# An encoder layer on one core: the parts of the first value column, gate2's way through DRAM, the last columns and the first loads are laid out anew

## The chip, the cores and the metric

The kernel runs on one core of a Trainium2 chip. The metric is the device time of one execution in microseconds (us). The core has TensorE (PE, with its weight loads as PEld), VectorE (DVE), ScalarE (ACT), GpSimd (POOL, hardly used here) and SyncE (SP). All DMAs of this kernel are issued by SP, in one order; an issue that has to wait holds all issues behind it.

## The reference

One layer of a bidirectional encoder, 256 tokens of width 2048, all in float32:

```
mod = SiLU(c) @ W_ada + b_ada -> shift1, scale1, gate1, shift2, scale2, gate2   (each 1 x 2048)
h = x * (1 + scale1) + shift1
x = LayerNorm(alpha * x + gate1 * Mixer(h))
h = x * (1 + scale2) + shift2
x = LayerNorm(alpha * x + gate2 * PEER(h))
```

The Mixer is an input projection, a bidirectional state-space scan beside a short gated convolution, and an output projection. PEER chooses 16 of 128 x 128 single-neuron experts per head by product keys; the kernel turns that into dense work: for each of 128 columns of 128 experts, u = h @ expert_u, a gate matrix G times gelu(u), and the sum over all columns of that product times expert_v.

## The kernel before

Float32 products are made of three matmuls on parts: a weight half (128x1024, 512 KB, "a raw half" in the text) is loaded into `raw`, ACT rounds it to `hi` (L78), and DVE takes the difference `lo` (L81). Each of raw, hi and lo has three buffers in the pool `stream`. A scheduler places each instruction by its priority, and weights are brought forward by a priority offset, so that loads run some halves ahead of their matmuls.

The stages in order of time, from the trace: adaLN's first two parts and the first quarter of the input projection (loads of w_ada and w_inA by turns), the rest of the Mixer, output projection and first LayerNorm, queries and the choice of experts, **expert_u** (128 columns, to 1815.6), **expert_v** (128 columns, 1817 to 2537), and the second LayerNorm (`finish`, to the end).

In expert_u the gates lie in GA, 128 columns as two tiles: columns below FIRST in one and the rest in the other. Each column's gelu is multiplied into its column of GA (L845). For expert_v a pair of columns is split into the parts ah and al (`a_pair`, L119 on ACT and L120 on DVE). These tiles are in a pool that takes over the memory of h2h and h2l, the parts of h that all matmuls of expert_u read. Each column is then 24 matmuls of 128x512 (L878 hi with ah, L879 hi with al, L881 lo with ah) over two halves, all into eight PSUM banks (two blocks of tokens by four blocks of 512 outputs) that are summed over all columns.

Beside expert_v run:

- sixteen steps of gate2 (`ada_step`): two loads of w_ada (512 KB each, tile `big`), a multiplication with row sum on DVE for each (L152), and at the end `ada_sum` (L158, L159) that makes a column of `mod` out of each step's sums. gate2 then stands with 128 values in each of 16 columns, across partitions, and is wanted as a row, the same on all partitions (`g2b`). It is stored to DRAM (`g_d`, L914) and loaded back as a broadcast (L915).
- the last LAST columns of expert_v, loaded into `big` and split into `old`, which takes over the memory of the first tile of GA. They are kept so that, at the end, the banks can be finished one after another, and a bank's `finish` (times g2b at L939, plus residual `ax` with row sum at L940, squares) can run beside the next bank's matmuls. The statistics of a block of 128 tokens, two more operations for each 512 outputs (L959, L960) and the store (L961) follow.

At the start, step d of the loop over 16 blocks of the width first loads adaLN's weights of step d + 1 (four loads, `ada_load`, L281), then splits two halves of w_inA and multiplies.

Of the kernel before, what the change touches and what calls it, by code (L numbers as in the profile page):

```python
# [34 lines left out]
LAG = 3  # L35
FIRST = 66
LAST = 4


@with_exitstack  # L40
def layer_kernel(ctx, tc, I, out, dbg=None):
# [27 lines left out]


    def wsplit(src, pool=stream, width=1024, ahead=600, after=None):

        with tc.high_priority(offset=ahead):
            raw = pool.tile([P, 1024], F32, name="raw", tag="raw", bufs=3)[:, :width]
            nc.sync.dma_start(raw, src)
            hi = pool.tile([P, 1024], F32R, name="hi", tag="hi")[:, :width]
            with tc.issue_after(after[0]) if after else nullcontext():
                A.activation(hi, raw, AF.Copy)  # L78
            lo = pool.tile([P, 1024], F32R, name="lo", tag="lo")[:, :width]
            with tc.issue_after(after[1]) if after else nullcontext():  # L80
                V.tensor_tensor(lo, raw, hi.bitcast(F32), op=ALU.subtract)  # L81
        c = lambda t: t.rearrange("p (k c) -> p k c", c=P)
        return c(hi), c(lo)
# [256 lines left out]
    V.memset(bones[:64, :64], 1.0)  # L340
    V.memset(bones[64:, 64:], 1.0)
    for d in range(ND):
        if d + 1 < ND:
# [6 lines left out]
        for half in range(2):  # L350
            wh, wl = wsplit(I["w_inA"][d, half], width=NA * 64, ahead=0)
            for i in range(NA // 2):
                k = half * NA // 2 + i
                mm3(first[k // 2][:, k % 2], wh[:, i], wl[:, i], h2h[:, d], h2l[:, d], False,
                    d == ND - 1 and k % 2 == 1)
            for _ in range(n // 2 if half == 0 else n - n // 2):
                unit_b(*units.pop(0))
# [437 lines left out]
    with ExitStack() as p4:  # L795
# [32 lines left out]
        with ExitStack() as p4a:  # L828
# [11 lines left out]
            for e2 in range(STAGE):  # L840
                nc.sync.dma_start(gel_d[e2], act_chunk(e2, wk, 1, step))
        wk = pool(p4, "wk4b")
        for e2 in range(STAGE, NE):
            ge = act_chunk(e2, wk, 2)
            behind = V.tensor_tensor(GA(e2)[:, 0], GA(e2)[:, 0], ge, op=ALU.mult).ins  # L845
            if e2 - STAGE < STAGE:
# [3 lines left out]
                with tc.issue_after(behind):  # L850
                    V.tensor_tensor(GA(k)[:, 0], GA(k)[:, 0], gb, op=ALU.mult)

    stR.close()


    with ExitStack() as p5:
# [41 lines left out]
        for e2 in range(NE - LAST):  # L898
            if e2 % 2 == 0:
                ah, al = a_pair(e2)  # L900
            if e2 == FIRST:
                old = gp.tile([P, FIRST, S], F32R, name="old", tag="GA0")
            for half in range(2):
                wh, wl = (w.rearrange("p k c -> p (k c)") for w in wsplit(I["expert_v"][e2, half]))
                for lo in range(2):
                    for j in range(2):
                        js = slice(j * 512, (j + 1) * 512)
                        for tb in range(2):
                            mm_v(tb, 2 * half + j, ah[:, e2 % 2], al[:, e2 % 2], wh[:, js], wl[:, js], lo, e2 == 0, False)
            if e2 % 6 == 5 and e2 < 96:  # L910
                ada_step(scb5, raw5[:2], 5, e2 // 6)
            if e2 == 100:
                ada_sum(5, slice(0, ND))
                nc.sync.dma_start(g2_d.rearrange("d p -> p d"), mod[:, 5])  # L914
                nc.sync.dma_start(g2b, bass.AP(tensor=g2_d.tensor, offset=g2_d.offset, ap=[[0, P], [1, D]]))  # L915
            if e2 >= 112:
                next(last, None)
# [5 lines left out]
        for rows, n, tag in ((lng, 0, "hi"), (lnb, 1, "lo")):  # L923
            for half in range(2):
                row = stream.tile([P, 1024], F32, name="lnrow", tag=tag)
                nc.sync.dma_start(row, bass.AP(tensor=I["ln2"].tensor, offset=I["ln2"].offset + n * D + half * 1024,
                                               ap=[[0, P], [1, 1024]]))
                rows += [row[:, :512], row[:, 512:]]

        def finish(tb):  # L930
# [3 lines left out]
            for c in range(4):  # L934
                r = rows5[tb][c]
                yield
                ax = stream.tile([P, 1024], F32, name="ax", tag="raw", bufs=3)[:, :512]
                nc.sync.dma_start(ax, ax_d[tb, :, c * 512:(c + 1) * 512])
                V.tensor_tensor(r, banks[tb][c], g2b[:, c * 512:(c + 1) * 512], op=ALU.mult)  # L939
# [95 lines left out]
```

## Time and profile before

| | before |
|---|---|
| median of three runs | 2547.92 us (2544.36 to 2559.14) |
| profiled execution | 2552.61 us |
| its span in the trace | 2550.7 us |
| mean clock granted to PE | 0.984 of full speed |
| PE busy | 2424.6 us, 95% of the span |
| DVE, ACT busy | 1862.2 us (73%), 1381.3 us (54%) |
| DMA queue with all loads and stores | 67.3% of 16 engines' time |

The span is the time from the first to the last instruction of the profiled execution; the profiled execution's own time has some 1.9 us around it. Times in views are in us from the start of the span. A row's "idle before" is what its engine waited just ahead of it, with the instruction that released it. The engine is busy when an instruction runs; matmuls overlap their successors, so the distance from one start to the next counts, which is 0.2285 us in the undisturbed value stage.

### The profile page before, as it was taken

How to read it: one execution, taken by the hardware profiler on the slowest of the kernel's cores; microseconds unless marked ns; L12 is line 12 of the kernel's file. 1: busy time of each engine (PE TensorE's matmuls, PEld its weight loads, DVE VectorE, ACT ScalarE, POOL GpSimd, SP SyncE). 2: the span in 40 equal slices, each digit the busy share in tenths (PEclk: the TensorE clock that was granted, in tenths of full speed). 3: DMA queues.
4: the chain of work that ended last, by engine and by line, in shares of the span. 5: the costliest groups of instructions: out<-in, count | busy, mean ns of one | idle time of the engine just before them, and what ended most of it. 6: DMA issues, size and time to landing. Idle time of an engine off the chain costs nothing.

```text
span 2550.7 us, 44290 instructions
## 1 busy us (share of the span) xinstructions
PE 2424.6 (95%) x17122; PEld 2248.3 (88%) x17122; DVE 1862.2 (73%) x3255; ACT 1381.3 (54%) x2506; POOL 0.9 (0%) x7
## 2 busy tenths in 40 slices
PE   5889999999999899999999999999998999999997
PEld 5889888888899799999999999999886888888886
DVE  8788888989887799898888855555675555645545
ACT  3435476656444554499999944444443444544442
POOL 0000000000000000000000000000000000000000
PEclk9999999999999899999999999999999999999999
DMA  9886766778887565355666666666788655655554
GB/s 356 313 297 236 260 217 224 235 260 280 267 291 259 196 206 181 116 181 193 199 195 200 198 218 219 218 217 219 257 307 274 217 194 190 223 192 193 193 190 149
DMA packets 183252, 575.67 MB, mean 226 GB/s; under 512 B 22209, under 2 KB 44929, under 8 KB 182657
## 3 DMA queue, kind: packets, MB, share of 16 engines
q1 hardware_dynamic: 183042, 572.85, 67.3%
q8 instruction: 134, 2.20, 0.3%
q14 instruction: 76, 0.62, 0.1%
HBM read 560.10 MB, written 12.66 MB: 225 GB/s over the span
## 4 chain that ended last, share of the span: by engine, by line
PE 67%; DMA 15%; DVE 12%; ACT 3%; issue 2%; SPq 1%; DVEq 0%; ACTq 0%
PE ps_u L91 9%; PE ps_u L92 9%; PE ps_u L93 9%; PE ps_v L879 8%; PE ps_v L881 8%; PE ps_v L878 8%; DVE lo L81 5%; DMA adaw<-in_w_ada_dram 4%; DMA raw<-in_w_in_dram 3%; DMA big<-in_w_ada_dram 2%; ACT hi L78 2%; DVE adaw L152 2%; DMA raw<-in_w_inA_dram 2%; PE ps_q L93 2%; PE ps_q L92 2%
## 5 line engine op out<-in xcount | busy, mean ns | idle before, releaser
L81 DVE TENSOR_TENSOR lo<-raw,hi 128x1024 fp32r<-128x1024 f32 (+1 forms) x804 | 972.1, 1212 | 506.8 <-ACT hi L78 504.7
L78 ACT ACTIVATE hi<-raw 128x1024 fp32r<-128x1024 f32 (+1 forms) x804 | 843.6, 1051 | 884.6 <-PE ps_v L879 302.1
L91 PE MATMUL ps_u<-h2h,hi 128*128 128x256 f32 x2048 | 568.7, 278 | 0.0
L92 PE MATMUL ps_u<-h2l,hi 128*128 128x256 f32 x2048 | 568.1, 277 | 0.0
L93 PE MATMUL ps_u<-h2h,lo 128*128 128x256 f32 x2048 | 568.1, 277 | 0.0
L878 PE MATMUL ps_v<-hi,ah 128*128 128x512 f32 x992 | 390.1, 393 | 9.9 <-ACT hi L78 8.1
L879 PE MATMUL ps_v<-hi,al 128*128 128x512 f32 x992 | 390.7, 394 | 1.2 <-DVE al L120 1.2
L91 PEld LDWEIGHTS ps_u<-h2h,hi 128*128 128x128 f32 x2048 | 386.2, 189 | 0.0
L92 PEld LDWEIGHTS ps_u<-h2l,hi 128*128 128x128 f32 x2048 | 384.6, 188 | 0.0
L93 PEld LDWEIGHTS ps_u<-h2h,lo 128*128 128x128 f32 x2048 | 384.5, 188 | 0.0
L881 PE MATMUL ps_v<-lo,ah 128*128 128x512 f32 x992 | 268.9, 393 | 0.8 <-DVE lo L81 0.8
L878 PEld LDWEIGHTS ps_v<-hi,ah 128*128 128x128 f32 x992 | 187.5, 189 | 52.3 <-ACT hi L78 8.9
L879 PEld LDWEIGHTS ps_v<-hi,al 128*128 128x128 f32 x992 | 187.7, 189 | 43.0 <-DVE al L120 1.6
L91 PE MATMUL ps_in<-h2h,hi 128*128 128x256 f32 x768 | 222.3, 289 | 3.0 <-DVE mod L159 2.2
L881 PEld LDWEIGHTS ps_v<-lo,ah 128*128 128x128 f32 x992 | 186.8, 189 | 42.0 <-DVE lo L81 2.0
L93 PE MATMUL ps_in<-h2h,lo 128*128 128x256 f32 x768 | 217.6, 283 | 2.3 <-DVE lo L81 2.3
L152 DVE SCALAR_TENSOR_TENSOR adaw<-adaw,scb 128x1024 f32<-128x1024 f32 x160 | 193.1, 1219 | 35.3 <-DMA adaw<-in_w_ada_dram 35.0
L92 PE MATMUL ps_in<-h2l,hi 128*128 128x256 f32 x768 | 217.6, 283 | 0.0
L809 ACT ACTIVATE o<-eq,gT 128x128 fp32r<-128x128 f32 x512 | 161.4, 388 | 0.0
L91 PEld LDWEIGHTS ps_in<-h2h,hi 128*128 128x128 f32 x768 | 146.6, 191 | 9.0 <-issue 4.2
L93 PEld LDWEIGHTS ps_in<-h2h,lo 128*128 128x128 f32 x768 | 147.1, 191 | 4.6 <-DVE lo L81 2.9
L93 PE MATMUL ps_o<-y,lo 128*128 128x256 f32 x512 | 145.6, 284 | 5.0 <-DVE lo L81 4.9
(285 smaller groups left out, 3975.0 us busy)
## 6 DMA issues: line engine op xcount, KB each, us to landing
raw<-in_expert_u_dram SPq DMA_DIRECT2D x256, 512.0 KB, 4.5
raw<-in_expert_v_dram SPq DMA_DIRECT2D x248, 512.0 KB, 3.9
adaw<-in_w_ada_dram SPq DMA_DIRECT2D x160, 512.0 KB, 6.0
raw<-in_w_in_dram SPq DMA_DIRECT2D x110, 512.0 KB, 5.0
raw<-in_w_out_dram SPq DMA_DIRECT2D x64, 512.0 KB, 4.3
raw<-in_w_query_dram SPq DMA_DIRECT2D x64, 512.0 KB, 3.9
raw<-in_w_inB_dram SPq DMA_DIRECT2D x44, 512.0 KB, 4.4
big<-in_w_ada_dram SPq DMA_DIRECT2D x32, 512.0 KB, 5.6
```

Of the source, the lines that this page charges most:

```text
L78: A.activation(hi, raw, AF.Copy)
L81: V.tensor_tensor(lo, raw, hi.bitcast(F32), op=ALU.subtract)
L91: T.matmul(ps, wh, mh, start=start, stop=False)
L92: T.matmul(ps, wh, ml, start=False, stop=False)
L93: T.matmul(ps, wl, mh, start=False, stop=stop)
L152: V.scalar_tensor_tensor(w, w, 0.5, scb[:, cs], op0=ALU.mult, op1=ALU.mult, accum_out=macc[:, half, part % 2, d:d + 1])
L809: A.activation(o2[:, k], eq[:, i, 1].bitcast(F32), AF.Copy, scale=gT[:, k, t0 + i:t0 + i + 1])
L878: T.matmul(banks[tb][c], ah[:, ts], vh, start=start, stop=False)
L879: T.matmul(banks[tb][c], al[:, ts], vh, start=False, stop=False)
L881: T.matmul(banks[tb][c], ah[:, ts], vl, start=False, stop=stop)
```

## The change

Five places are edited.

1. The first tile of GA holds 98 columns instead of 66 (FIRST), and 6 columns instead of 4 (LAST) are kept for the end; their loads begin at column 110 instead of 112.
2. Column 0 of GA is split into tiles of its own, a0h and a0l, at column 72 of expert_u (STAGE is 64), in a pool of their own. Column 0 of expert_v uses these.
3. gate2 is summed step by step and stored in sixteen stores of 128 elements, each written one step behind its sum; the broadcast load comes at column 104.
4. The residual `ax` is loaded in four loads of 128x1024 ahead of `finish`, in place of eight of 128x512 within it.
5. The first two halves of w_inA are loaded ahead of the loop, and so ahead of adaLN's weights of step 1.

```diff
@@ -33,8 +33,8 @@
 TURNS = (0, 1, 7, 2, 8), (3, 9, 4, 10, 5, 11, 6), (12, 13, 14, 15)
 WHOLE = range(3, 43, 3)
 LAG = 3
-FIRST = 66
-LAST = 4
+FIRST = 98
+LAST = 6
 
 
 @with_exitstack
@@ -68,11 +68,16 @@
     lnp = const.tile([P, 2, ND], F32, name="lnp")
 
 
+    def wload(src, pool=stream, width=1024):
+        raw = pool.tile([P, 1024], F32, name="raw", tag="raw", bufs=3)[:, :width]
+        nc.sync.dma_start(raw, src)
+        return raw
+
     def wsplit(src, pool=stream, width=1024, ahead=600, after=None):
 
         with tc.high_priority(offset=ahead):
-            raw = pool.tile([P, 1024], F32, name="raw", tag="raw", bufs=3)[:, :width]
-            nc.sync.dma_start(raw, src)
+            raw = src if pool is None else wload(src, pool, width)
+            pool = pool or stream
             hi = pool.tile([P, 1024], F32R, name="hi", tag="hi")[:, :width]
             with tc.issue_after(after[0]) if after else nullcontext():
                 A.activation(hi, raw, AF.Copy)
@@ -339,6 +344,7 @@
     V.memset(bones, 0.0)
     V.memset(bones[:64, :64], 1.0)
     V.memset(bones[64:, 64:], 1.0)
+    raws = [wload(I["w_inA"][0, half], width=NA * 64) for half in range(2)]
     for d in range(ND):
         if d + 1 < ND:
             ada_load(d + 1)
@@ -348,7 +354,8 @@
             units += [(d // 4 - 1, u) for u in range(NB // 2)]
         n = -(-len(units) // (4 - d % 4))
         for half in range(2):
-            wh, wl = wsplit(I["w_inA"][d, half], width=NA * 64, ahead=0)
+            wh, wl = (wsplit(raws[half], None, NA * 64, 0) if d == 0 else
+                      wsplit(I["w_inA"][d, half], width=NA * 64, ahead=0))
             for i in range(NA // 2):
                 k = half * NA // 2 + i
                 mm3(first[k // 2][:, k % 2], wh[:, i], wl[:, i], h2h[:, d], h2l[:, d], False,
@@ -839,6 +846,7 @@
 
             for e2 in range(STAGE):
                 nc.sync.dma_start(gel_d[e2], act_chunk(e2, wk, 1, step))
+        a0 = pool(ctx, "a0")
         wk = pool(p4, "wk4b")
         for e2 in range(STAGE, NE):
             ge = act_chunk(e2, wk, 2)
@@ -849,6 +857,10 @@
                 nc.sync.dma_start(gb, gel_d[k])
                 with tc.issue_after(behind):
                     V.tensor_tensor(GA(k)[:, 0], GA(k)[:, 0], gb, op=ALU.mult)
+            if e2 == STAGE + 8:
+
+                a0h, a0l = (a0.tile([P, S], F32R, name=n) for n in ("a0h", "a0l"))
+                split(a0h, a0l, GA(0)[:, 0])
 
     stR.close()
 
@@ -898,6 +910,7 @@
         for e2 in range(NE - LAST):
             if e2 % 2 == 0:
                 ah, al = a_pair(e2)
+            ahs, als = (a0h, a0l) if e2 == 0 else (ah[:, e2 % 2], al[:, e2 % 2])
             if e2 == FIRST:
                 old = gp.tile([P, FIRST, S], F32R, name="old", tag="GA0")
             for half in range(2):
@@ -906,14 +919,17 @@
                     for j in range(2):
                         js = slice(j * 512, (j + 1) * 512)
                         for tb in range(2):
-                            mm_v(tb, 2 * half + j, ah[:, e2 % 2], al[:, e2 % 2], wh[:, js], wl[:, js], lo, e2 == 0, False)
-            if e2 % 6 == 5 and e2 < 96:
-                ada_step(scb5, raw5[:2], 5, e2 // 6)
-            if e2 == 100:
-                ada_sum(5, slice(0, ND))
-                nc.sync.dma_start(g2_d.rearrange("d p -> p d"), mod[:, 5])
+                            mm_v(tb, 2 * half + j, ahs, als, wh[:, js], wl[:, js], lo, e2 == 0, False)
+            if e2 % 6 == 5 and e2 < 102:
+                d = e2 // 6
+                if d:
+                    nc.sync.dma_start(g2_d[d - 1:d].rearrange("d p -> p d"), mod[:, 5, d - 1:d])
+                if d < ND:
+                    ada_step(scb5, raw5[:2], 5, d)
+                    ada_sum(5, slice(d, d + 1))
+            if e2 == 104:
                 nc.sync.dma_start(g2b, bass.AP(tensor=g2_d.tensor, offset=g2_d.offset, ap=[[0, P], [1, D]]))
-            if e2 >= 112:
+            if e2 >= NE - 3 * LAST:
                 next(last, None)
         for _ in last:
             pass
@@ -926,6 +942,12 @@
                 nc.sync.dma_start(row, bass.AP(tensor=I["ln2"].tensor, offset=I["ln2"].offset + n * D + half * 1024,
                                                ap=[[0, P], [1, 1024]]))
                 rows += [row[:, :512], row[:, 512:]]
+        axs = []
+        for tb in range(2):
+            for half in range(2):
+                ax = stream.tile([P, 1024], F32, name="ax", tag="hi" if tb and half else "raw", bufs=3)
+                nc.sync.dma_start(ax, ax_d[tb, :, half * 1024:(half + 1) * 1024])
+                axs += [ax[:, :512], ax[:, 512:]]
 
         def finish(tb):
 
@@ -934,8 +956,7 @@
             for c in range(4):
                 r = rows5[tb][c]
                 yield
-                ax = stream.tile([P, 1024], F32, name="ax", tag="raw", bufs=3)[:, :512]
-                nc.sync.dma_start(ax, ax_d[tb, :, c * 512:(c + 1) * 512])
+                ax = axs[4 * tb + c]
                 V.tensor_tensor(r, banks[tb][c], g2b[:, c * 512:(c + 1) * 512], op=ALU.mult)
                 V.scalar_tensor_tensor(r, r, 1.0, ax, op0=ALU.mult, op1=ALU.add, accum_out=s[:, c:c + 1])
                 if c == 0:
```

**PE at the seam of the two stages.** ps_u is the last matmul of expert_u; hi and lo are parts of expert_v's weights. PE's order before:

```order
L93 MATMUL ps_u<-h2h,lo 128x256
L878 MATMUL ps_v<-hi,ah 128x512
L879 MATMUL ps_v<-hi,al 128x512
L878 MATMUL ps_v<-hi,ah 128x512
L879 MATMUL ps_v<-hi,al 128x512
```

PE's order after, from the same place, and where column 1 begins:

```order
L98 MATMUL ps_u<-h2h,lo 128x256
L890 MATMUL ps_v<-hi,a0h 128x512
L891 MATMUL ps_v<-hi,a0l 128x512
...
L893 MATMUL ps_v<-lo,a0h 128x512 x4
L890 MATMUL ps_v<-hi,ah 128x512
L891 MATMUL ps_v<-hi,al 128x512
```

The first 24 matmuls read a0h and a0l in place of ah and al; the order of matmuls is otherwise the same. On ACT the ah of the first pair stands behind the last gelu in both; before, three pairs follow each other there, and after, one, a hi, and then two.

**SP around gate2's store and load.** `big` is a load of w_ada (step of gate2) or of a last column, `raw` a half of expert_v. SP's order before:

```order
L75 DMA raw<-in_expert_v_dram 128x1024 x2
L163 DMA big_23146<-in_w_ada_dram 128x1024
L75 DMA raw<-in_expert_v_dram 128x1024
L893 DMA big_23146<-in_expert_v_dram 128x1024
L75 DMA raw<-in_expert_v_dram 128x1024 x2
L914 DMA g_d<-mod 128x16x1
L893 DMA big_23146<-in_expert_v_dram 128x1024
L75 DMA raw<-in_expert_v_dram 128x1024 x2
L915 DMA g2b<-g_d 128x2048
L75 DMA raw<-in_expert_v_dram 128x1024 x2
```

SP's order after, at the end of the sixteen steps:

```order
L926 DMA g_d<-mod 128x1
L168 DMA big_23153<-in_w_ada_dram 128x1024
L73 DMA raw<-in_expert_v_dram 128x1024 x2
L926 DMA g_d<-mod 128x1
L168 DMA big_23153<-in_w_ada_dram 128x1024
L73 DMA raw<-in_expert_v_dram 128x1024 x2
L905 DMA big_23153<-in_expert_v_dram 128x1024
L73 DMA raw<-in_expert_v_dram 128x1024
L926 DMA g_d<-mod 128x1
L905 DMA big_23153<-in_expert_v_dram 128x1024
L73 DMA raw<-in_expert_v_dram 128x1024 x2
L931 DMA g2b<-g_d 128x2048
```

The one store of sixteen columns has become sixteen of one, each a few raw halves behind the second load of its step. From the first to the last load of w_ada in this stage SP issues 42 raw halves before and 50 after. The load g2b stands ten raw halves later than before.

**SP at the start.** `adaw` are adaLN's weights, `raw` halves of w_inA. SP's order before:

```order
L296 DMA sc_d<-scb 1x2048
L281 DMA adaw_189<-in_w_ada_dram 128x1024 x2
L281 DMA adaw_192<-in_w_ada_dram 128x1024 x2
L75 DMA raw<-in_w_inA_dram 128x768 x2
L281 DMA adaw_252<-in_w_ada_dram 128x1024 x2
L281 DMA adaw_255<-in_w_ada_dram 128x1024 x2
L75 DMA raw<-in_w_inA_dram 128x768 x2
```

SP's order after:

```order
L301 DMA sc_d<-scb 1x2048
L73 DMA raw<-in_w_inA_dram 128x768 x2
L286 DMA adaw_193<-in_w_ada_dram 128x1024 x2
L286 DMA adaw_196<-in_w_ada_dram 128x1024 x2
L286 DMA adaw_252<-in_w_ada_dram 128x1024 x2
L286 DMA adaw_255<-in_w_ada_dram 128x1024 x2
L73 DMA raw<-in_w_inA_dram 128x768 x2
```

The first two halves have moved past four loads of adaLN's weights, and nothing else has.

## Rows read from the trace of the kernel before

**Rows 1.** The page: busy time by engine, the chain's shares, loads with us to landing
```profile
PE 2424.6 (95%) x17122; PEld 2248.3 (88%) x17122; DVE 1862.2 (73%) x3255; ACT 1381.3 (54%) x2506; POOL 0.9 (0%) x7
...
PE 67%; DMA 15%; DVE 12%; ACT 3%; issue 2%; SPq 1%; DVEq 0%; ACTq 0%
...
raw<-in_expert_v_dram SPq DMA_DIRECT2D x248, 512.0 KB, 3.9
```

**Rows 2.** Windows: us; busy us (and instructions) by engine, PE's clock, DMA share, GB/s
```profile
35.00:100.00 65.00, 55.94 (x423) 52.90 (x424) 51.37 (x82) 29.91 (x52) 0.00 (x0) 0.95 0.90 332
1200.00:1760.00 560.00, 560.00 (x4891) 560.00 (x4890) 394.04 (x571) 379.77 (x830) 0.00 (x0) 1.00 0.65 208
1826.00:1945.00 119.00, 118.22 (x515) 96.15 (x514) 89.47 (x111) 49.16 (x52) 0.00 (x0) 1.00 0.89 306
1950.00:2000.00 50.00, 41.92 (x175) 33.74 (x174) 23.66 (x26) 18.93 (x20) 0.00 (x0) 0.93 0.74 241
2000.00:2200.00 200.00, 200.00 (x875) 164.09 (x875) 109.17 (x101) 94.22 (x99) 0.00 (x0) 1.00 0.61 202
```

**Rows 3.** Timeline of PE at the seam: start, us, instruction, idle before
```profile
1815.37 0.28 PE L93 MATMUL ps_u<-h2h,lo 128*128 128x256 f32 x1
1817.46 0.51 PE L878 MATMUL ps_v<-hi,ah 128*128 128x512 f32 x1 [1.82 <-ACT ah L119]
1819.20 0.80 PE L879 MATMUL ps_v<-hi,al 128*128 128x512 f32 x1 [1.24 <-DVE al L120]
...
1825.33 0.40 PE L879 MATMUL ps_v<-hi,al 128*128 128x512 f32 x1
```

**Rows 4.** Timeline of ACT at the seam
```profile
1812.85 1.06 ACT L78 ACTIVATE hi<-raw 128x1024 fp32r<-128x1024 f32 x1 [1.39 <-PE ps_u L92]
...
1816.79 1.66 ACT L119 ACTIVATE ah<-GA 128x512 fp32r<-128x512 f32 x3
```

**Rows 5.** Timeline of DVE at the seam
```profile
1818.46 1.89 DVE L120 TENSOR_TENSOR al<-GA,ah 128x512 fp32r<-128x512 f32 x3
```

**Rows 6.** Timeline of SP's queue around gate2's store
```profile
1954.47 0.39 SPq L914 DMA_DIRECT2D g_d<-mod  x1
...
1958.68 0.86 SPq L75 DMA_DIRECT2D raw<-in_expert_v_dram  x2
1966.54 0.33 SPq L915 DMA_DIRECT2D g2b<-g_d  x1
```

**Rows 7.** DMA issues of 1940 to 1980: KB each, us to landing
```profile
g_d<-mod SPq DMA_DIRECT2D x1, 8.0 KB, 12.1
```

**Rows 8.** The chain that ended last, two of its pieces
```profile
1958.68 12.12 DMA raw<-in_expert_v_dram
...
2536.54 2.96 DMA ax<-ax_d
```

**Rows 9.** Timeline of PE behind the store
```profile
1972.02 0.80 PE L878 MATMUL ps_v<-hi,ah 128*128 128x512 f32 x1 [5.62 <-ACT hi L78]
```

**Rows 10.** Waits of SP's queue, 1826 to 1945: us in total, times, longest
```profile
SPq L75 <- DVE lo L81: 73.0, 40, 4.3
```

**Rows 11.** Lines of DVE, forms apart: busy us, mean ns, idle before
```profile
L120 DVE TENSOR_TENSOR old<-big,old 128x1024 fp32r<-128x1024 f32 x8 | 9.6, 1219 | 0.3 <-ACT old L119 0.3
...
L158 DVE TENSOR_TENSOR mod<-macc 128x1 f32<-128x1 f32 x48 | 7.3, 152 | 0.5
```

**Rows 12.** Timeline of DVE at the end
```profile
2537.60 0.68 DVE L940 SCALAR_TENSOR_TENSOR big<-big,ax 128x512 f32<-128x512 f32 x1
...
2539.59 0.69 DVE L940 SCALAR_TENSOR_TENSOR big<-big,ax 128x512 f32<-128x512 f32 x1 [1.30 <-DMA ax<-ax_d]
```

**Rows 13.** Timeline of PE at the start
```profile
20.88 0.58 PE L91 MATMUL ps<-h2h,hi 128*128 128x256 f32 x1 [16.78 <-ACT hi L78]
```

**Rows 14.** Timeline of SP's queue at the start
```profile
9.45 3.41 SPq L281 DMA_DIRECT2D adaw<-in_w_ada_dram  x4
13.53 0.81 SPq L75 DMA_DIRECT2D raw<-in_w_inA_dram  x2
```

## The prediction, made before the result was known

> **What bounds the kernel now.** I read the page first: TensorE (PE) is busy 2424.6 us of a span of 2550.7, and the chain that ended last is two thirds PE, with DMA 15% and VectorE (DVE) 12% [rows 1]. So a microsecond counts only where PE stands still or runs slowly. The windows say where: in the expert_u stage 1200 to 1760 and in the value stage 2000 to 2200 PE is busy without a gap (875 matmuls in 200 us, 0.2285 us each), while 1950 to 2000 has only 175 matmuls and 8.1 us idle, and in 35 to 100 it is the DMA engines that are 0.90 busy and PE 56 of 65 us [rows 2]. What the change touches is therefore priced at the gaps and not by busy times. Next I read PE's own timeline at the two gaps, then the engines that release it there, then the end and the start.
>
> The profiled execution took 2552.6 us, 1.9 more than its span; the median of the runs is 2547.9. I make the sum against the profiled one and move it to the median by the difference, 4.7.
>
> **The seam between expert_u and expert_v.** PE's last ps_u matmul starts at 1815.37. The first value matmul needs ah and starts at 1817.46 after 1.82 us idle, the next needs al and starts at 1819.20 after 1.24 more; then matmuls are slow, as the 0.80 of the second shows, until the one at 1825.33, which has the 0.40 of the stage's other matmuls [rows 3]. From the end of ps_u to there fifteen matmuls took 1825.33 − 1815.65 = 9.7 us; at full spacing 15 × 0.229 = 3.4. The seam costs **6.2 us**, half of it waiting, half the lower clock behind the wait. What is late is the split of the first gate pairs: ah stands on ScalarE (ACT) behind the last hi and the last gelu and runs at 1816.79 [rows 4], al on DVE at 1818.46 behind lo and the two products [rows 5]. It can't be earlier in the kernel before, since these tiles lie in h2h's memory, which PE reads until 1815.6.
>
> The change gives column 0 parts of its own, split at column 72 of expert_u. The 24 matmuls of column 0 then need only hi and lo of the first two halves, and the second hi ran at 1812.85 [rows 4]. They last 24 × 0.229 = 5.5 us, to 1821.1, and column 1 needs the pair's ah and al from there on: these ran by 1818.5 and 1820.4 [rows 4, 5], and nothing is put ahead of them, so they are on time with more than 0.7 us to spare. The one extra split of 128x256 falls into the expert_u stage, where PE is fed without a gap and DVE works 394 and ACT 380 of 560 us [rows 2]: nothing. I take **−6.2**, with 0 as the other end if another wait holds the first matmul as long (the banks, which the last gelu frees just ahead of ah at 1816.79 [rows 4]; then some 1 us idle and part of the slow clock stay, about 3).
>
> **gate2 turned and read back.** Before, one store of 2048 elements of 4 bytes is issued at 1954.47 and lands 12.1 us later [rows 6, 7], at 1966.57, and from 1959.54 on SP stands idle until it issues the broadcast load at 1966.54 [rows 6]: 7.0 us. A raw half issued behind the store, at 1958.68, lands 12.12 us later [rows 8], three times the 3.9 us of this stage's median raw [rows 1]. PE waits for hi, 5.62 us of it up to 1972.02 [rows 9], and then goes slowly: 175 matmuls in 50 us where 219 fit, 44 × 0.2285 = **10.0 us** lost. The change stores 128 elements at a time, one column of sixteen, spread over the stage; the last stands as far ahead of the broadcast load in SP's order as the whole store did (one load of a last column and two raw halves between them). A sixteenth of the elements at the same rate is 12.1 / 16 = 0.76 us. The load itself, 1 MB, stays, and the raws around it run with the lead that the rest of the stage has. So −10.0.
>
> What do sixteen stores cost? Each is one more issue on SP (0.39 us [rows 6]) and waits for its sum of gate2, and the raw loads are queued behind it. In 1826 to 1945 SP is no free engine: it waits 73.0 us for raw buffers to be released by DVE's lo [rows 10], although PE is held up for only 0.8 of 119 us [rows 2]. Counted in SP's order, a step's two w_ada loads have 42 / 16 = 2.6 raw halves with them before and 50 / 16 = 3.1 after. PE uses a half in 12 × 0.2285 = 2.74 us, so a step could last 7.2 us before (119 / 16 = 7.4 is what it took) and may last 8.6 after. What SP loses to a store (0.4, and some waiting for a sum that stands a few raws behind its loads) overlaps the waits for buffers that it has anyway. PE's lead is two to three halves, about 7 us. I take **+2**, with 0 and +11 as ends (0.7 us in each step). The 32 small sums of 0.152 us [rows 11] lie in DVE's gaps.
>
> The Trainium skill speaks against this part: "DMA: Bandwidth & Descriptors", section "Rules for kernel authors", wants many small transfers coalesced into one large, since under 64 KB one pays mostly overhead; the same page's "Anatomy of one DMA" gives about 2.0 us fixed cost per DMA on its software path, so by an estimate from that page 16 × 2 = 32 us if each were exposed, and the sum would turn to +22 for this part. That rule holds for a DMA that somebody waits for; the row shows the one large store already landing as late as 12.1 us for 8 KB, and its waiter is what the change removes.
>
> **The end.** Before, DVE's last product with the residual waits 1.30 us for ax, which is loaded only when a buffer comes free, at 2536.54, and lands 2.96 us later; the one before it stands at 2537.60 [rows 8, 12]. With the residuals loaded ahead of it, the last product needs only the last bank's multiplication, and takes the place at about 2537.7 where the one before it stands now, instead of 2539.59: **−1.9** (at least the 1.3 that the row shows as idle). The statistics, the eight products and the stores behind stay. Six columns instead of four finish bank by bank: the same matmuls in another order. Their 12 splits of 1.22 us on DVE [rows 11] fit beside lo in a half of 2.74 us, as eight did before with PE full at 2000 to 2200 [rows 2]. A bank has 18 matmuls, 4.1 us, in which DVE's two operations of 0.7 us fit. Gates in 98 and 30 columns instead of 66 and 62 are the same copies, on the PE-bound stretch: nothing.
>
> **The start.** Before, PE starts at 20.88 [rows 13], when the first two raw halves, issued at 13.53 behind four loads of w_ada (from 9.45) [rows 14], have come through ACT. The change issues the two first: PE could start near 16, 4.9 us earlier. But the DMA engines are 0.90 busy over 35 to 100 and PE is not [rows 2], and the second step's raws come behind the same bytes in either order. 4.9 us of earlier work then become 4.9 us of waiting for them: **0**, with −5 and +1 as ends.
>
> **Sum:** −6.2 − 10.0 + 2 − 1.9 + 0 = **−16.1**: 2552.6 − 16.1 = 2536.5 for the profiled execution, and 2531.8 against the median: **2532 us**.
>
> **Rivals.**
> The start edit keeps its gain: if what bounds the first 100 us is not DMA but PE (56 busy of 65 us [rows 2]), 4.9 more: 2527. Against it the DMA share of 0.90. Chance 0.15.
> The value stage's ada steps starve PE: if each step is 0.7 us beyond PE's pace, −16.1 − 2 + 11 = −7: 2541. For it SP's 73.0 us of waits; against it the lead and the longer steps. Chance 0.2.
> The seam only moves: the banks or hi hold PE there as before or half as long, and 3 to 6 come back: 2535 to 2538. Chance 0.15.
> Slower: a small store costs nearly what the large one does, because its landing time is latency and not elements (12.1 us for 8 KB says neither), and raws behind it on the same DMA queues wait as the one at 1958.68 did. It decides at one place: the steps. Each store must hold the raws up by more than (18.1 + 7) / 16 = 1.6 us, the lead counted, to use up the gain, and by 2.4 us to be slower by 0.5%; at the full 12 us it would cost up to 16 × 12.1 = 194 us. At 3 us it gives 16 × 3 − 7 − 18.1 = +23: 2571. Chance 0.06.
> The forecast itself: 0.44.
>
> Half a per cent, 12.7 us, is about what a measurement of this kernel can tell from none. Faster by more needs all but 3.4 us of the sum: the forecast, the start's rival and a third of the seam's, less the part of the forecast's own spread of some 4 us that falls below: 0.60. Same: 0.34. Slower: 0.06. The range goes from the start's gain with an ada phase at nothing (2548 − 23 = 2525) to the starved steps (2541) and a little beyond: **2524 to 2543**.
>
> **What would show it.** The value stage's first matmul less than 0.3 us behind the last ps_u, at spacing 0.229; SP's wait for gate2's store gone and 219 matmuls in each 50 us around the broadcast load; PE's idle between 1820 and 1950 within 3 us; DVE's last residual product without idle ahead; PE's first matmul near 16 but the same matmul count by 100 us. It would be wrong if SP's waits on the sums of gate2 or the landing of raws in the ada steps (5 us now) grew by more than 2 us a step, or if PE's early start stayed to the end of the in-projection.

## The result and the profile after

The changed kernel takes **2623.34 us** (median of 6 runs, 2613.27 to 2632.82) against 2550.64 of the kernel before (6 runs): **1.0287 times as long, 95% interval 1.0254 to 1.0319**. The forecast was 2532 us. The profiled execution took 2613.27 us; its span is 2611.5, 60.8 more than before.

The page of the changed kernel (busy times, chain, two loads with their median landing) answers to [rows 1]:

```profile
PE 2453.8 (94%) x17122; PEld 2260.9 (87%) x17122; DVE 1873.0 (72%) x3286; ACT 1377.8 (53%) x2507; POOL 0.9 (0%) x7
...
PE 63%; DMA 17%; DVE 13%; ACT 4%; issue 2%; SPq 0%; DVEq 0%; ACTq 0%
...
raw<-in_expert_v_dram SPq DMA_DIRECT2D x244, 512.0 KB, 3.4
...
big<-in_w_ada_dram SPq DMA_DIRECT2D x32, 512.0 KB, 10.3
```

PE is busy 29 us longer with the same 17122 matmuls. The loads of w_ada for gate2 land after 10.3 us in the median, where the page of before has 5.6:

```profile
big<-in_w_ada_dram SPq DMA_DIRECT2D x32, 512.0 KB, 5.6
```

The page's median raw of this stage even fell from 3.9 to 3.4. The chain now has 17% DMA. The windows, the answer to [rows 2], say where:

```profile
35.00:100.00 65.00, 55.59 (x422) 53.70 (x422) 51.58 (x83) 29.61 (x52) 0.00 (x0) 0.92 0.88 322
1480.00:1780.00 300.00, 300.00 (x2650) 300.00 (x2649) 172.35 (x223) 131.94 (x166) 0.00 (x0) 1.00 0.68 218
1826.00:1945.00 119.00, 95.12 (x361) 73.43 (x360) 62.33 (x91) 34.45 (x37) 0.00 (x0) 0.90 0.91 201
1950.00:2000.00 50.00, 36.33 (x135) 27.79 (x135) 25.28 (x37) 14.27 (x15) 0.00 (x0) 0.90 0.99 214
2100.00:2200.00 100.00, 100.00 (x431) 80.98 (x430) 48.74 (x46) 42.83 (x45) 0.00 (x0) 1.00 0.57 186
```

In 1826 to 1945, the stretch of gate2's steps, PE ran 361 matmuls where it ran 515 before, and DMA moved 201 GB/s at a share of 0.91, where it had moved 306 at 0.89. DMA engines that are busy and move less: that is the row to remember. The stretch goes on to 2060, since each step takes longer, so 1950 to 2000 shows it as well (214 GB/s at 0.99). PE's waits from 1815 to the end (total us, times, longest):

```profile
PE ps_v L890 <- ACT hi L83: 26.6, 9, 4.9
PE ps_v L893 <- DVE lo L86: 23.2, 10, 4.0
```

PE waits for hi and lo, that is, for raws. The two rows make 49.8 us without work; behind the waits PE also runs more slowly (in 1826 to 1945 a granted clock of 0.90, where it was 1.00 before [rows 2]). The chain (start, us, what) shows what a step looks like:

```profile
1866.77 0.33 SPq L73
...
1867.15 0.43 SPq L926
...
1867.63 13.72 DMA big<-in_w_ada_dram
...
1881.37 0.07 DVE big L157
...
1885.59 12.28 DMA big<-in_w_ada_dram
```

Right behind gate2's store, issued at 1867.15, stands a load of w_ada which lands 13.72 us later; DVE multiplies, SP issues the next load at 1885.59, and that one takes 12.28. The stores' own landing in the changed kernel:

```profile
DMA to landing us min/median/max: 6.6/8.9/13.4
```

A store of 512 bytes lands in 8.9 us in the median. The whole store of 8 KB took 12.1 [rows 7]. That points at the stores; the experiments test it. Counted over the value stage: the first group of lo matmuls starts at 1811.36, the last of the streamed columns at 2565.13, with 243 halves between them, which at the undisturbed 2.743 us a half (12 × 200 / 875 [rows 2]) are 666.5 us; 753.8 passed, **87 us too many**. Before the same count gives 14 (1822.36 to 2513.89, 247 halves). Of the 87, 77 pass until 2062, while gate2 is on its way, and 10 behind it, at a slower pace of PE that the section on the hardware comes back to. The 60.8 us of the span are these 73 more in the stage, less 5 at the seam and 2 at the end (both below), and less 6 that the profile is ahead when expert_u starts (1065.2 against 1071.5; over the profiles of all kernels here this start lies between 1065.2 and 1073.8).

The rest went as forecast. The seam on PE's timeline, the answer to [rows 3]:

```profile
1809.42 0.28 PE L98 MATMUL ps_u<-h2h,lo 128*128 128x256 f32 x1
1809.53 0.39 PE L890 MATMUL ps_v<-hi,a0h 128*128 128x512 f32 x1
1809.76 0.40 PE L891 MATMUL ps_v<-hi,a0l 128*128 128x512 f32 x1
```

The first value matmul follows the last ps_u after 0.11 us, and the first lo group starts 1.9 us behind it (before 7.0), without slow matmuls in between:

```profile
1811.36 0.84 PE L893 MATMUL ps_v<-lo,a0h 128*128 128x512 f32 x3
```

The end on DVE's timeline, the answer to [rows 12]: the last product with the residual follows its multiplication without a wait for ax, and the statistics begin 1.5 us after the last matmul ended, at 2601.32 (before 2536.95 to 2540.32, 3.4).

```profile
2599.86 0.69 DVE L960 TENSOR_TENSOR big<-ps_v,g2b 128x512 f32<-128x512 f32 x1 [2.77 <-PE ps_v L893]
2600.59 0.69 DVE L961 SCALAR_TENSOR_TENSOR big<-big,ax 128x512 f32<-128x512 f32 x1
...
2601.32 0.16 DVE L966 TENSOR_REDUCE st<-st 128x1 f32<-128x4 f32 x1
```

The start on PE's timeline, the answer to [rows 13]: the first matmul at 17.18 in place of 20.88, and then a wait for the second step's raws until 28.14 (27.96 before).

```profile
17.18 0.58 PE L96 MATMUL ps<-h2h,hi 128*128 128x256 f32 x1 [13.09 <-ACT hi L83]
...
28.14 0.39 PE L96 MATMUL ps<-h2h,hi 128*128 128x256 f32 x1 [4.24 <-ACT hi L83]
```

### The profile page after: what moved, and what is told of

Read it like the earlier page. It is cut to its first block, busy times and chain, and to the rows that moved or that the text cites. A ratio compares the mean times of both kernels' runs of the same rounds, so it can differ in the third digit from the quotient of the medians.

```text
span 2611.5 us, 44324 instructions
## 1 busy us (share of the span) xinstructions
PE 2453.8 (94%) x17122; PEld 2260.9 (87%) x17122; DVE 1873.0 (72%) x3286; ACT 1377.8 (53%) x2507; POOL 0.9 (0%) x7
## 4 chain that ended last, share of the span: by engine, by line
PE 63%; DMA 17%; DVE 13%; ACT 4%; issue 2%; SPq 0%; DVEq 0%; ACTq 0%
PE ps_u L97 9%; PE ps_u L96 9%; PE ps_u L98 9%; PE ps_v L890 7%; PE ps_v L891 7%; PE ps_v L893 7%; DMA big<-in_w_ada_dram 5%; DVE lo L86 5%; DMA adaw<-in_w_ada_dram 4%; DMA raw<-in_w_in_dram 3%; DVE adaw L157 3%; ACT hi L83 3%; PE ps_q L97 2%; PE ps_q L98 2%; PE ps_q L96 2%
## 6 DMA issues: line engine op xcount, KB each, us to landing
big<-in_w_ada_dram SPq DMA_DIRECT2D x32, 512.0 KB, 10.3
```

## The experiments

All ratios are to the kernel before on the same chip, with 95% intervals. They are worked out from the single runs, so they need not be the quotient of the two medians beside them.

| kernel | median us | before | ratio |
|---|---|---|---|
| e1 changed, one store | 2546.99 | 2549.99 | 0.9976 (0.9958 to 0.9994) |
| e2 before, sixteen stores alone | 2616.44 | 2549.99 | 1.0257 (1.0230 to 1.0284) |
| e3 before, blind stores | 2617.90 | 2549.99 | 1.0281 (1.0243 to 1.0320) |
| e4 changed, one store, late load | 2549.05 | 2549.99 | 0.9998 (0.9976 to 1.0020) |
| e5 blind, elements 512 bytes apart | 2554.15 | 2555.37 | 0.9996 (0.9966 to 1.0025) |
| e6 blind, one row | 2552.44 | 2555.37 | 0.9985 (0.9959 to 1.0012) |
| e7 blind, 128 rows of 512 bytes | 2552.84 | 2555.37 | 0.9994 (0.9968 to 1.0021) |
| e8 changed, gate2 turned on DVE | 2544.02 | 2555.37 | 0.9935 (0.9905 to 0.9965) |
| e9 blind, elements 64 bytes apart | 2544.92 | 2551.39 | 0.9975 (0.9953 to 0.9997) |
| e10 before, gate2 turned on DVE alone | 2537.92 | 2551.39 | 0.9937 (0.9912 to 0.9962) |
| e11 before, seam alone | 2540.38 | 2551.39 | 0.9957 (0.9935 to 0.9979) |
| e12 before, start alone | 2549.71 | 2551.39 | 0.9997 (0.9979 to 1.0015) |
| e13 before, seam, e10, residuals | 2533.63 | 2561.19 | **0.9898** (0.9858 to 0.9938) |
| e14 before, columns alone | 2552.24 | 2561.19 | 0.9977 (0.9942 to 1.0011) |

### Which edit costs the time: e1 and e2

Theory 1 says that the sixteen stores cost the time; its rival, that another edit does. e1 is the changed kernel with gate2's way of before, e2 the kernel before with the new way.

```diff
-                d = e2 // 6
-                if d:
-                    nc.sync.dma_start(g2_d[d - 1:d].rearrange("d p -> p d"), mod[:, 5, d - 1:d])
-                if d < ND:
-                    ada_step(scb5, raw5[:2], 5, d)
-                    ada_sum(5, slice(d, d + 1))
-            if e2 == 104:
+                ada_step(scb5, raw5[:2], 5, e2 // 6)
+            if e2 == 100:
+                ada_sum(5, slice(0, ND))
+                nc.sync.dma_start(g2_d.rearrange("d p -> p d"), mod[:, 5])
```

> The changed kernel with gate2's way put back: one sum, one store of 128x16 and the broadcast load right behind it; the other four edits stay. Theory 1 (the sixteen small stores cost the time) gives 2550.6 - 6.2 (seam) - 1.9 (end) = 2542 us, with PE idle under 2 us from 1815 to 1940. The rival that another edit costs it (the six last columns, the start, the residual loads) leaves it at 2600 or more.

> The kernel before with only the sixteen stores, each behind its sum. Theory 1 gives the whole loss without the gains of seam and end: 2623 + 8 = 2631 us, or 1.03 of before. The rival that the loss comes only together with another edit gives 2541 to 2552.

e1 came out at 0.9976 (2547 us where 2542 was expected), and e2 (the same lines with + and - exchanged, on the kernel before) at 1.0257. The new way of gate2 accounts for the loss, with or without the other edits; the rival falls.

### Waits of the queue or the transfers: e3

The stores could cost because SP stands on their sums, with the raws queued behind it, or because their transfers are in the way. e3 keeps the kernel before whole and adds sixteen stores of a constant to DRAM that nobody reads. They have no sum to wait for.

```diff
+    xx_d = dram.tile([ND, P], F32, name="xx_d")
...
-                ada_step(scb5, raw5[:2], 5, e2 // 6)
+                h = ada_step(scb5, raw5[:2], 5, e2 // 6)
+                d = e2 // 6
+                with tc.issue_after(h.ins), tc.high_priority(offset=300):
+                    nc.sync.dma_start(xx_d[d:d + 1].rearrange("d p -> p d"), badaT[:, 5, d:d + 1])
```

> The kernel before, whole, with sixteen more stores of 128 elements of four bytes into DRAM that nobody reads, from a constant, one behind the second load of each step of gate2. They wait for no sum, so SP is held only for 16 issues of 0.4 us. Theory 1a (the transfers themselves hold up the loads behind them) gives +60 to +90: 2610 to 2640 us, with loads of 512 KB landing after 9 us or more. Theory 1b (SP is held by the stores' waits for sums, 63 us of waits on mod in the changed kernel) gives 2551 to 2558 us, with landings near 5 us.

+68 us by the medians: theory 1a, the transfers. 67.9 / 16 = 4.2 us of lost PE time for each store of 512 bytes. The stores of the changed kernel cost some 9 us more than that: e2 is 66 us above the kernel before although the one large store, worth 10, is gone from it. Part of those 9 may be SP's waits for the sums (63 us of waits on mod in the changed kernel, most of them hidden); no run separates them. The windows of two us in e3's profile, around one of the stores (issued at 1882.73 behind three loads, landed 15.8 us later, the latest of the sixteen):

```profile
1890.00:1892.00 2.00, 2.00 (x7) 1.52 (x6) 1.80 (x4) 1.06 (x1) 0.00 (x0) 0.50 0.91 365
1892.00:1894.00 2.00, 2.00 (x6) 1.61 (x5) 1.84 (x3) 0.00 (x0) 0.00 (x0) 0.50 1.38 51
1894.00:1896.00 2.00, 2.00 (x8) 1.57 (x8) 0.00 (x0) 0.00 (x0) 0.00 (x0) 0.81 0.83 57
1896.00:1898.00 2.00, 1.33 (x6) 0.75 (x4) 0.00 (x0) 1.00 (x2) 0.00 (x0) 1.00 0.92 88
1898.00:1900.00 2.00, 1.89 (x8) 1.60 (x9) 1.83 (x2) 0.74 (x3) 0.00 (x0) 1.00 0.90 162
```

At 1890 to 1892 DMA moves 365 GB/s, then for six us 51, 57 and 88, at a mean share of 1.04: the engines are occupied and little gets through. (The share counts a packet's whole time in the window in which it begins, so in so short a window it can pass 1.) In windows of one us, the same profile has such a hole, four to eight us below 120 GB/s, for each of the sixteen stores. The raws and the w_ada loads that are queued behind it pay. The landings of e3's stores:

```profile
DMA to landing us min/median/max: 8.3/9.3/15.8
```

### What in the transfer costs: e5, e6, e7 and e9

e3 has 128 elements of 4 bytes from 128 partitions, side by side in 512 bytes of DRAM. Three properties could matter: that it is a small store at all, that it has 128 pieces or pieces of 4 bytes, or that the pieces are neighbours. Each kernel changes one of them in e3's lines.

```diff
 e5: elements 512 bytes apart
+    xx_d = dram.tile([ND, P, 128], F32, name="xx_d")
+                    nc.sync.dma_start(xx_d[d, :, :1], badaT[:, 5, d:d + 1])
 e6: the same 512 bytes as one row from one partition
+                    nc.sync.dma_start(xx_d[d:d + 1], iota[:1])
 e7: 128 rows of 512 bytes
+    xx_d = dram.tile([ND, P, 128], F32, name="xx_d")
+                    nc.sync.dma_start(xx_d[d], iota)
 e9: elements 64 bytes apart
+    xx_d = dram.tile([ND, P, 16], F32, name="xx_d")
+                    nc.sync.dma_start(xx_d[d, :, :1], badaT[:, 5, d:d + 1])
```

> As e3 (the kernel before with sixteen more blind stores of 128 four-byte elements, +68 us there), but the 128 elements of a store lie 512 bytes apart in DRAM instead of side by side. If the elements of a store hold each other up because they fall into the same 512 bytes, this gives +0 to +15: 2551 to 2565 us and loads at full rate. If every four-byte element of a store costs, wherever it lies, it gives +60 to +80 as e3.

> As e3, but each of the sixteen blind stores writes the same 512 bytes as one row from one partition. If four-byte elements are what costs, +0 to +7 (16 issues of 0.4 us): 2551 to 2557 us. If any small store between the loads costs its 4 us whatever its elements, +60: 2611 us.

> As e3, but each blind store writes 128 rows of 512 bytes, 64 KB: as many rows as e3 has elements, 128 times the bytes. If rows of 512 bytes go at the rate of the loads, 64 KB cost 0.2 us of transfer each and the time is 2551 to 2557 us. If it is the number of 128 pieces per store that costs, +60: 2611 us or more.

> As e3 and e5, with the 128 four-byte elements of each blind store 64 bytes apart (0 apart in e3: +68 us; 512 bytes apart in e5: nothing). If elements hold each other up when they share 512 bytes, some of the loss is back: eight elements share 512 bytes here, +4 to +20. If they must share 64 bytes or less, nothing: within 0.4% of before, landings of the stores near 4.6 us as in e5.

None of the four costs anything measurable: by the upper end of its interval e5, the slowest, could cost 0.25%, which is 0.4 us a store where e3 has 4.2. (e9's interval lies wholly below 1, which nothing in its edit explains; differences of this size are not to be built on.) e6 rules out the small store as such, e7 the 128 pieces, e5 the four-byte element: as many elements, of the same size, from the same partitions and in the same place of the queue are free when they lie 512 bytes apart, and by e9 also at 64. What costs is that they are **neighbours** in DRAM. The two us windows of e5 around its store at 1888.99 have no hole, and in windows of one us neither e5 nor e9 has more than a single us below 120 GB/s until its last blind store is through:

```profile
1890.00:1892.00 2.00, 2.00 (x10) 1.66 (x9) 2.00 (x3) 0.65 (x1) 0.00 (x0) 1.00 0.94 297
1892.00:1894.00 2.00, 2.00 (x10) 1.65 (x9) 1.58 (x2) 0.59 (x2) 0.00 (x0) 1.00 0.92 301
1894.00:1896.00 2.00, 2.00 (x11) 1.63 (x10) 1.18 (x3) 0.89 (x1) 0.00 (x0) 1.00 0.72 248
```

The landings in e5, and then in e9, which halve those of e3:

```profile
DMA to landing us min/median/max: 3.4/4.6/6.0
```

```profile
DMA to landing us min/median/max: 3.4/4.6/6.7
```

Where between 4 and 64 bytes the border lies wasn't measured. That the engines which carry neighbouring partitions hold each other up at one piece of memory would explain the rows (high shares, little moved, gone at 64 bytes), but is an argument, not shown.

Here the Trainium skill and the measurement part. "DMA: Bandwidth & Descriptors", section "Specifications", says that transfers below 512 bytes cause a read-modify-write and miss the line rate, and its "Rules for kernel authors" says that under 64 KB one pays mostly overhead. Both point against the change, and the change did lose. But small transfers as such are not what lost here: e5 and e9 have elements of 4 bytes and e6 stores of 512 bytes, and beside the loads of this kernel they cost nothing that can be measured. The runs decide, and they put the cost on the neighbourhood.

### Where gate2's ten microseconds were: e4, e8 and e10

e4 takes SP's wait for the one store away: the broadcast load stands fourteen raw halves behind the store and not two. The cut is against e1; the lines that collect the loads are left out.

```diff
+            if e2 == 34:
+                ahead = loads[-1]
             if e2 == 100:
                 ada_sum(5, slice(0, ND))
                 nc.sync.dma_start(g2_d.rearrange("d p -> p d"), mod[:, 5])
-                nc.sync.dma_start(g2b, bass.AP(tensor=g2_d.tensor, offset=g2_d.offset, ap=[[0, P], [1, D]]))
+                with tc.issue_after(ahead.ins):
+                    nc.sync.dma_start(g2b, bass.AP(tensor=g2_d.tensor, offset=g2_d.offset, ap=[[0, P], [1, D]]))
```

> The changed kernel with one store of 128x16 after all sums, and the broadcast load tied behind the raw half of column 34, some fourteen halves behind the store (two before), so that SP doesn't stand on the store. If before lost 10 us to SP's wait, this gives 2542 - 10 = 2532 us and no SP wait on the store. If the loss came from the store's transfer in front of the raws and not from SP's wait, the gap stays in part: 2536 to 2542.

0.9998, no better than e1, and 2549 us where 2532 was expected if the wait was the cause and 2536 to 2542 if not. (e1, e4 and e8 all came out some 5 us or more above what was expected; the last section has a slower pace in their profiles.) SP no longer stands on the store, and PE still loses 8.8 us around it (three halves of 3.32, 9.98 and 3.78 us). The windows show the same hole as in e3, with the one store of 2048 elements:

```profile
1974.00:1976.00 2.00, 2.00 (x11) 1.63 (x10) 1.19 (x1) 0.00 (x0) 0.00 (x0) 1.00 0.87 332
1976.00:1978.00 2.00, 2.00 (x10) 1.67 (x9) 0.39 (x1) 1.48 (x2) 0.00 (x0) 1.00 0.79 98
1978.00:1980.00 2.00, 2.00 (x10) 1.63 (x10) 1.44 (x2) 0.10 (x1) 0.00 (x0) 1.00 0.51 21
1980.00:1982.00 2.00, 1.72 (x8) 1.12 (x7) 0.32 (x1) 1.06 (x1) 0.00 (x0) 1.00 1.03 53
1982.00:1984.00 2.00, 2.00 (x10) 1.60 (x10) 0.91 (x1) 0.00 (x0) 0.00 (x0) 1.00 0.56 27
1984.00:1986.00 2.00, 0.75 (x4) 0.28 (x2) 0.00 (x0) 0.00 (x0) 0.00 (x0) 1.00 0.58 100
1986.00:1988.00 2.00, 0.00 (x0) 0.00 (x0) 0.00 (x0) 0.00 (x0) 0.00 (x0) 1.00 0.90 322
```

For ten us 98, 21, 53, 27 and 100 GB/s. The chain there (the store's issue, the next load's issue and a raw behind it) gives the loss to what stands behind the store in the queue and not to SP's wait for its landing:

```profile
1972.65 0.43 SPq L931
...
1973.13 4.34 SPq L907
...
1977.57 11.28 DMA raw<-in_expert_v_dram
```

SP needs 4.34 us for the issue of the load of a last column right behind the store, which takes it 0.33 just ahead of the store, and the raw behind that lands after 11.28 us.

e8 avoids the scattered elements: mod is turned on DVE in blocks of 32 x 32, and gate2 goes to DRAM in four stores of 16 rows of 128 bytes. e10 is the same on the kernel before, and the cut is e10's.

```diff
+        sq = wk.tile([P, 32], F32, name="sq")
+        sqT = wk.tile([P, 32], F32, name="sqT")
+        V.memset(sq, 0.0)
...
             if e2 == 100:
                 ada_sum(5, slice(0, ND))
-                nc.sync.dma_start(g2_d.rearrange("d p -> p d"), mod[:, 5])
+                V.tensor_copy(sq[:, :ND], mod[:, 5])
+                V.transpose(sqT, sq)
+                for b in range(4):
+                    nc.sync.dma_start(g2_d[:, 32 * b:32 * b + 32], sqT[32 * b:32 * b + ND])
```

> The changed kernel with one sum, then gate2 turned on DVE in blocks of 32 x 32, and stored in four stores of 16 rows of 128 bytes in place of 2048 elements of four bytes; then the broadcast load. If four-byte elements are what costs, the stretch around the store keeps its 219 matmuls in 50 us, and the time is that of e1 less 9: 2538 us. If small stores cost by their number, four of them cost 16 us and it is 2555 us.

> The kernel before with gate2's way of e8 alone (turned on DVE, four stores of 16 rows of 128 bytes). The stretch around the old store lost 10 us of PE; they come back: 2550 - 10 = 2540 us, ratio 0.996. If e8's gain came from its other edits, ratio 1.000.

0.9935 (2544 us where 2538 was expected) and 0.9937 (2538, expected 2540): the hole is gone. e8's window of the stretch that lost 44 matmuls before [rows 2]:

```profile
1950.00:2000.00 50.00, 50.00 (x220) 41.03 (x219) 32.30 (x37) 22.64 (x24) 0.00 (x0) 1.00 0.88 300
```

220 matmuls in 50 us, at 300 GB/s. The two operations on DVE (here in e13) cost next to nothing:

```profile
L929 DVE STREAM_TRANSPOSE sqT<-sq 128x32 f32<-128x32 f32 x1 | 0.2, 214 | 0.0
L928 DVE COPY sq<-mod 128x16 f32<-128x16 f32 x1 | 0.2, 178 | 0.0
```

### The other edits: e11, e12, e14, and all that help: e13

e11 has only the tiles a0h and a0l with their split and use, e12 only the raws ahead of the loop, e14 only FIRST 98 and LAST 6. Of e11 and e12 one line each is shown.

```diff
 e11
...
+            ahs, als = (a0h, a0l) if e2 == 0 else (ah[:, e2 % 2], al[:, e2 % 2])
...
 e12
...
+    raws = [wload(I["w_inA"][0, half], width=NA * 64) for half in range(2)]
...
 e14
-FIRST = 66
-LAST = 4
+FIRST = 98
+LAST = 6
```

> The kernel before with column 0's parts in tiles of their own alone. Theory of the prediction: no wait between ps_u and ps_v, 6.2 us less: ratio 0.9976. In three of the four profiles with this edit the expert_u stage took 757 us and not 744 as in all six without it: if the edit brings the slower pace of PE there with it, the ratio is 1.000 to 1.003 and the profile shows 757 us.

> The kernel before with the first two halves of w_inA loaded ahead of adaLN's weights alone. The prediction has 0: PE starts near 17 but waits for the second step's halves to 28 as before; ratio 0.999 to 1.001, first matmul of the in-projection's second part at 250 to 258 us as in the other profiles. The rival that the start keeps its gain: 5 us less, ratio 0.998.

> The kernel before with FIRST 98 and LAST 6 alone. The prediction has 0 for it: ratio 1.000, expert_u in 744 us. If the slower pace comes with this edit, in half of the runs or more: expert_u in 757 us in the profile, a spread of runs of 20 us, ratio 1.002 to 1.005.

e11: 0.9957, a gain of 0.21% to 0.65% by its interval, near the edge of what such runs can tell; the forecast 6.2 us (0.24%) lies within. e12: 0.9997. Its interval doesn't quite shut out the rival's 0.998; its profile does, with PE starting at 17.07 and waiting to 28.00, where it stood at 27.96 before. e14: 0.9977, not told apart from zero, with expert_u at its usual pace.

e13 is the kernel before with e11, e10 and the residuals loaded ahead. The cut has one or two lines of each.

```diff
+            ahs, als = (a0h, a0l) if e2 == 0 else (ah[:, e2 % 2], al[:, e2 % 2])
...
+                V.transpose(sqT, sq)
...
-                ax = stream.tile([P, 1024], F32, name="ax", tag="raw", bufs=3)[:, :512]
-                nc.sync.dma_start(ax, ax_d[tb, :, c * 512:(c + 1) * 512])
+                ax = axs[4 * tb + c]
```

> The kernel before with three edits: column 0's parts apart, gate2 turned on DVE and stored in four stores of rows, the residuals loaded ahead. FIRST 66, LAST 4 and the start are those of before. By the parts, 6.2 + 10 + 1.9 = 18 us less: ratio 0.993. If the slower pace of PE in expert_u that e1, e4 and e8 show comes with the 98 and 30 columns, this kernel shows 744 us there and a spread of runs of 10 us, not 20, and a ratio of 0.990 to 0.993; if it comes with column 0's parts, 757 us and 0.995.

0.9898 (0.9858 to 0.9938), 2533.63 us: faster than the kernel before and than the changed one. The expectation of 0.993 lies inside the interval. The median is 28 us below that of before, more than the 18 of the parts; but before stood at 2561 here, 6 to 11 us above its medians on the other chips.

## Why the prediction was wrong

**The seam, −6.2: right.** No gap, no slow matmuls; the first lo group stands 1.9 us behind the last ps_u in place of 7.0, from there to the next lo group it is 2.7 us in place of 4.1, and e11 gained.

**gate2's store, −10.0: the place and size right, the cause half right.** The prediction named SP's wait and the late raw behind the store side by side, and counted on both to go with the size of the store. e4 took only the wait away, and 8.8 us stayed, where before lost 10.2 (the two halves around the store before lasted 5.49 and 10.23 us where 2.74 each is usual); what held PE was the raw, kept up by the store's transfer and by the slow issue behind it. e10 got it back by changing the elements' layout (0.9937, 0.24% more than the ten, which lie just inside its interval).

**The sixteen stores, +2: wrong, and this is the step that failed.** "A sixteenth of the elements at the same rate is 12.1 / 16 = 0.76 us." The time doesn't go with the elements: 128 neighbours land in 8.9 us where 2048 elements took 12.1, and e3's windows show six us at 51 to 88 GB/s for a store with a sixteenth of the elements. Each store cost 4.2 us of PE after everything that hides it (e3), and the changed kernel lost 77 us by 2062 where the sum had 2. The working also left out what it had in hand: the row of the raw that landed 12.12 us after its issue [rows 8] showed that a raw behind a store is held up, and the step priced only SP's issue and its wait for a sum. e3 has no wait for a sum and costs 68 us.

The **rival "Slower"** had the main part of this (the landing time is not elements; the raws behind a store wait as the one at 1958.68 did), and its turning point of 1.6 to 2.4 us a store was passed by far. Its reason, a latency of every small store, is not what the runs show: the stores of e5 and e9 are as small, land in 4.6 us and cost nothing measurable. It was given 0.06, because a duration seen once, 12.1 us for 2048 elements, was read as a rate. A single row can't tell a fixed cost from a cost by the piece; the range should have held both ends, 0.76 and 12.1 us, as the rival did with its 194 us. The rule of the Trainium skill that was weighed and set aside there, in "DMA: Bandwidth & Descriptors", section "Rules for kernel authors", had the right sign, and the estimate of 32 us from that page was nearer than the 2 of the sum; that is partly luck, since e5, e6 and e9 have as many small stores for nothing.

**The end, −1.9: right.** The statistics start 1.5 us behind the last matmul and not 3.4. **The start, 0: right**, by e12 and the profiles, in which PE is at the same place by 28 us. **The columns, 0: right** as far as e14 tells.

**What the parts leave over.** The changed kernel is 7 us slower than e2 by the medians, where its other edits should make it 8 faster. e1, e4 and e8, the kernels with all four other edits, show in their profiles a slower pace of PE in expert_u that costs 13 us, and the changed kernel's profile shows one in expert_v that costs 10. The profiles of e11, e12 and e14, with one of these edits each, don't have it, nor has e13's, which has the residuals loaded ahead. Each kernel has a single profile, so whether the combination makes it likelier or chance did is open.

## What to carry to other kernels

Before a store is cut into pieces or turned by its access pattern, look at what its elements are in DRAM: neighbours of 4 bytes from many partitions held the transfers of this kernel to 21 to 100 GB/s for 6 us a store (128 elements, e3) or 10 us (2048, e4), while rows, or 128 elements 64 bytes apart, cost nothing measurable. Turn such a vector on an engine first (DVE took 0.2 us) and store rows. And when a trace shows an operation once, its duration is a point, not a rate: price a smaller one between "in proportion" and "the same", and look at what lands late behind it rather than at the wait of the queue that issued it.

## What the runs showed of the hardware that was not expected

**A DMA share near 1 with little moved.** In 1950 to 2000 of the changed kernel the engines were 0.99 busy at 214 GB/s, and elsewhere the same load runs at 300 GB/s with 0.88 (e8). The share alone doesn't say that bandwidth is used.

**Two paces of PE at the same granted clock of 1.00.** In the uniform half of expert_u the changed kernel runs 2650 matmuls from 1480 to 1780 (windows above), as do the profiles of all kernels here but three (2649 or 2650); e1 runs 2550 in the same stretch, without idle time, as e4 (2549) and e8 (2550) do:

```profile
1480.00:1780.00 300.00, 300.00 (x2550) 300.00 (x2549) 165.44 (x212) 127.05 (x160) 0.00 (x0) 1.00 0.63 210
```

Expert_u took 757 us there (1066.9 to 1824.2) and 744 in the changed kernel (1065.2 to 1809.1). The changed kernel has the like in expert_v: 431 matmuls in 2100 to 2200 against 438 before, 2.80 us a half from 2058, where PE came out of its last wait, to the end of the streamed columns, where before has 2.747. Both come to 4.4 ns more from one matmul to the next (300 / 2550 against 300 / 2650; 2.80 / 12 against 2.747 / 12), though the matmuls differ in size. The pace can part within a stage: from 1400 to 1440 the changed kernel runs 348 matmuls and e1 347, from 1480 to 1520 they run 356 and 342. No run here shows what chooses it.
